# Six load buffers in place of three for the second MLP product, a last group of four pairs, and the output scale row made earlier

## The chip, the cores and the metric

The kernel runs on one core of a Trainium2 chip. The time is device microseconds of one execution. TensorE does the matrix products, VectorE and ScalarE the elementwise work, GpSimd issues accumulating DMAs, and SyncE issues the plain DMAs. [...]

## The reference, cut to what matters

One decoder layer for 512 tokens of width 1024, in float32. The change touches its last part, the MLP and its residual:

```python
h = rmsnorm(x, g_pre_ffn[l]) * (1.0 + sc2) + sh2
u = jax.nn.relu(h @ w_ff1[l])            # 512 x 4096
y = (u * u) @ w_ff2[l]                   # 512 x 1024
x = x + ga2 * rmsnorm(y, g_post_ffn[l])  # ga2: gate from w_ada and c
```

## The kernel before, in words

A product of two float32 matrices is made of three matmuls: each operand is split into a high part (float32r, copied by ScalarE) and a low part (the rest, subtracted by VectorE), and high x high, high x low and low x high are added in PSUM. `split` (line 112) is this pair of instructions.

The first product of the MLP, h @ w_ff1, takes 32 slabs of w_ff1 (tile `st`, 128x1024, a ring of three slots shared with all earlier loads), 24 matmuls each. Its squared results stay in SBUF as 16 blocks (`ub`). In the same loop, `ada_cols` computes the last eight columns of the gate; after the loop, `rows_of` (line 149) makes the row `ga2b` (gate times post-norm gain) out of them with eight transposes on TensorE into the two banks "tr", and VectorE copies the banks to SBUF.

The second product, (u*u) @ w_ff2, is the seven-product stage. It goes over 16 pairs of w_ff2 slabs. A pair is a 2 x 2 block matrix on both sides (two halves of the tokens, two slabs; two halves of the columns), and a scheme of seven products in place of eight is used, with sums of blocks as operands. It has two phases.

First phase: for each pair p, four products into the accumulators p1, p5, p6, p7 (two PSUM banks each; p1 has the banks "tr"), 24 matmuls. `first_ops(p)` makes the operands: the split of four token blocks (`ah`), the two column halves of slab 2p (`x`, loaded by `load(p)`), and a sum n. `w_right[p]` holds the right column halves of both slabs of the pair, and n is that plus x. For p = 0 to 2 (`BY_DVE`) the slab `w_right[p]` is loaded plainly and VectorE adds x to it (line 879); for p > 2 `column_sums(p)` (line 865) lets ScalarE copy x to a tile `wn` and GpSimd add `w_right[p]` to it with an accumulating DMA. `ah` has two tiles, one for even and one for odd pairs, and the weights `whi` and `wlo` four slots (`WBUF`), two for each pair. So the operands of pair p + 1 are made while TensorE multiplies pair p.

Second phase: three more products for each pair, 18 matmuls, onto the same accumulators. `fourth_sum(p)` (line 899) adds a half slab to a block with an accumulating DMA; `second_ops(p)` (line 902) splits the slab 2p + 1 (`w`), three token blocks (`a`) and that sum (`n`, a tile `wn`). The last `LAST` = 3 pairs are taken in another order: result tile by result tile (p7 for tokens 2 and 3, then p5 and p1 for tokens 0, then 1). As each of the six tiles is done, `piece` (line 996) takes it up on VectorE (L1001 adds, L1005 multiplies with `ga2b`) and ScalarE (square with a sum), and `end` (line 1012) applies the norm, adds the residual and stores.

Inside the stage the order on TensorE, VectorE, ScalarE and GpSimd is the order of the code (`manual_schedule`), and SyncE issues its loads in one queue, each waiting for its slot. An instruction that waits holds up all that is behind it on its engine. The program sets aside a part of SBUF for the descriptors of GpSimd's DMAs; before, its size is left at the default.

## Time and profile before

| | us |
|---|---|
| median of three runs | 801.88 (801.0 to 801.96) |
| profiled execution | 802.46 |
| its span, first to last instruction | 800.5 |
| TensorE busy | 767.6 (96%), 4014 matmuls |
| VectorE busy | 593.9 (74%) |
| ScalarE busy | 415.0 (52%) |
| mean granted clock | 0.993 |

A busy TensorE is one with matmuls in its pipe. The chain of work that ended last gives 71% of the span to TensorE, 17% to VectorE and 7% to DMA. Shares over the whole span hide that stages differ, so the rows below are read by stage. The w_ff1 product ends at about 631 us, the first phase of the seven-product stage goes from there to about 726 us, the second to the last matmul at 791.4 us.

### The profile page before, as it was taken

Reading aid. Unit: us, or ns where it says so; the run is one execution under the profiler, and the core shown is the slowest. Engines: PE = TensorE matmul, PEld = TensorE weight load, DVE = VectorE, ACT = ScalarE, POOL = GpSimd, SP = SyncE. Lnnn points to the kernel's source line nnn. Section 1 sums busy time; section 2 is a strip of 40 time slices with the busy share of each in tenths; the row PEclk is TensorE's granted clock in tenths of the full one; section 3 lists DMA queues with packets and bytes.
Section 4 is the critical chain, followed back from the end, with each engine's and each line's share of the span. In section 5 each row is a group of like instructions: output and inputs, shape, how many; then the busy total and the mean of one; then the engine's idle time right before and its main releaser. Section 6 shows DMA issues by size and latency. Waiting matters only on the chain.

```text
span 800.5 us, 10875 instructions
## 1 busy us (share of the span) xinstructions
PE 767.6 (96%) x4014; PEld 638.4 (80%) x4014; DVE 593.9 (74%) x1112; ACT 415.0 (52%) x752; POOL 28.3 (4%) x44
## 2 busy tenths in 40 slices
PE   5999999998899999998999999999999989999995
PEld 5889977667889887786788898888888858888884
DVE  6876799999957578678875964655544668887966
ACT  6555666554546668623245852232232258777852
POOL 0000000000000000000000000000000011142000
PEclk9999999999999999999999999999999999999998
DMA  9933201112122210377883234444332269899622
GB/s 352 386 121 106 79 27 54 54 63 95 55 82 77 80 54 27 102 247 247 271 298 123 79 130 133 141 150 137 128 103 71 74 150 211 204 195 268 198 77 105
DMA packets 32598, 111.18 MB, mean 139 GB/s; under 512 B 3873, under 2 KB 3873, under 8 KB 32545
## 3 DMA queue, kind: packets, MB, share of 16 engines
q1 hardware_dynamic: 28224, 99.44, 36.3%
q0 software_dynamic: 4176, 11.01, 8.2%
q8 instruction: 31, 0.51, 0.3%
q14 instruction: 23, 0.18, 0.1%
q10 hardware_dynamic: 144, 0.03, 0.0%
HBM read 108.38 MB, written 2.10 MB: 138 GB/s over the span
## 4 chain that ended last, share of the span: by engine, by line
PE 71%; DVE 17%; DMA 7%; issue 2%; ACT 2%; SPq 0%; DVEq 0%; ACTq 0%
PE mm L140 25%; PE s L140 19%; PE o L140 6%; PE s L858 6%; PE mm L858 5%; PE tr L858 4%; DMA st<-in_ada_dram 3%; DVE wlo L114 3%; DVE a L486 3%; DVE isc L412 2%; DVE sm L411 2%; DMA st<-in_w_gate_dram 2%; PE tr L430 2%; DVE be L488 1%; PE tr L140 1%
## 5 line engine op out<-in xcount | busy, mean ns | idle before, releaser
L113 ACT ACTIVATE whi<-st 128x1024 fp32r<-128x1024 f32 (+3 forms) x119 | 117.4, 989 | 170.8 <-DMA st<-in_w_up_dram 45.0
L114 DVE TENSOR_TENSOR wlo<-st,whi 128x1024 fp32r<-128x1024 f32 (+3 forms) x119 | 134.8, 1135 | 65.4 <-ACT whi L113 65.2
L140 PE MATMUL mm<-hTh,whi 128*128 128x512 f32 x192 | 78.2, 407 | 0.1
L140 PE MATMUL mm<-hTh,wlo 128*128 128x512 f32 x192 | 75.3, 392 | 0.0
L140 PE MATMUL mm<-hTl,whi 128*128 128x512 f32 x192 | 75.1, 391 | 0.0
L140 PE MATMUL mm<-whi,hTh 128*128 128x256 f32 (+2 forms) x208 | 62.6, 307 | 0.0
L213 DVE CUSTOM_DVE_ANT_0 st<-st,cb,vec 128x1024 f32<-128x1024 f32 x32 | 40.9, 1283 | 27.7 <-DMA st<-in_ada_dram 27.7
L140 PE MATMUL mm<-wlo,hTh 128*128 128x256 f32 (+2 forms) x208 | 60.5, 297 | 0.0
L140 PE MATMUL mm<-whi,hTl 128*128 128x256 f32 (+2 forms) x208 | 60.5, 297 | 0.0
L140 PE MATMUL s<-h2h,whi 128*128 128x512 f32 (+1 forms) x120 | 43.4, 361 | 0.0
L140 PE MATMUL s<-h2l,whi 128*128 128x512 f32 (+1 forms) x120 | 43.3, 361 | 0.0
L140 PE MATMUL s<-h2h,wlo 128*128 128x512 f32 (+1 forms) x120 | 43.3, 361 | 0.0
L140 PEld LDWEIGHTS mm<-hTh,wlo 128*128 128x128 f32 x192 | 36.0, 188 | 7.7
L140 PEld LDWEIGHTS mm<-hTh,whi 128*128 128x128 f32 x192 | 36.2, 189 | 6.6 <-DVE qT L524 0.3
L140 PEld LDWEIGHTS mm<-hTl,whi 128*128 128x128 f32 x192 | 36.2, 188 | 6.2
L140 PEld LDWEIGHTS mm<-wlo,hTh 128*128 128x128 f32 x208 | 40.0, 192 | 1.1
L140 PEld LDWEIGHTS mm<-whi,hTl 128*128 128x128 f32 x208 | 39.9, 192 | 0.6
L140 PEld LDWEIGHTS mm<-whi,hTh 128*128 128x128 f32 x208 | 39.5, 193 | 0.4
L858 PE MATMUL s<-whi,ah 128*128 128x512 f32 x100 | 36.3, 393 | 0.0
L114 DVE TENSOR_TENSOR ah<-ub,ah 128x1024 fp32r<-128x1024 f32 (+1 forms) x17 | 20.5, 1208 | 18.1 <-ACT ah L113 18.1
L140 PE MATMUL s<-kT,qT 128*128 128x256 f32 (+2 forms) x128 | 30.9, 346 | 2.1 <-ACT be L485 1.8
L868 POOL DMA_DIRECT2D wn<-in_w_right_dram x13 | 11.4, 876 | 594.3 <-ACT wn L867 551.2
(352 smaller groups left out, 1947.1 us busy)
## 6 DMA issues: line engine op xcount, KB each, us to landing
st<-in_w_ff_dram SPq DMA_DIRECT2D x64, 512.0 KB, 3.5
st<-in_ada_dram SPq DMA_DIRECT2D x32, 512.0 KB, 4.3
sa<-in_ada_dram SPq DMA_DIRECT2D x16, 512.0 KB, 8.2
st<-in_w_gate_dram SPq DMA_DIRECT2D x16, 512.0 KB, 3.3
wn<-in_w_right_dram POOLq DMA_DIRECT2D x13, 512.0 KB, 5.5
st<-in_w_first_dram SPq DMA_DIRECT2D x8, 512.0 KB, 8.7
st<-in_w_b_dram SPq DMA_DIRECT2D x8, 512.0 KB, 3.3
st<-in_w_a_dram SPq DMA_DIRECT2D x8, 512.0 KB, 3.2
```

What stands on the lines that cost most here:

```text
L113: nc.scalar.activation(dst_hi, src, AF.Copy)
L114: nc.vector.tensor_tensor(dst_lo, src, dst_hi.bitcast(F32), op=ALU.subtract)
L140: nc.tensor.matmul(o, lhsT, rhs, start=start, stop=stop)
L213: nc.vector.tensor_tensor_reduce(out=st, in0=st, in1=cb[0], scale=1.0, scalar=vec[:, j:j + 1], op0=ALU.mult, op1=ALU.add, accum_out=mod[:, ...
L411: nc.vector.max(out=m8, in_=cur)
L412: nc.vector.match_replace(out=cur, in_to_replace=m8, in_values=cur, imm_value=SENT)
L430: nc.tensor.transpose(tr[:, j * P:(j + 1) * P], ps[e][:, j * P:(j + 1) * P], ident)
L486: nc.vector.tensor_tensor_scan(a[:, n - 1::-1], a[:, n - 1::-1], zero.to_broadcast([P, n]), 1.0, op0=ALU.mult, op1=ALU.add)
L488: nc.vector.tensor_tensor(be[:, :n - 1], be[:, :n - 1], a[:, 1:n], op=ALU.mult)
L858: nc.tensor.matmul(acc[i], s[:, ts], m[:, cs], start=f, stop=l, skip_group_check=onto)
L868: nc.gpsimd.dma_start(nw[p], w_right[p], accum_op=ALU.add)
```

## The change

`w_right[0..2]` and the w_ff2 slabs now alternate between the old ring `st` (three slots) and a new ring `ld` (three slots) through `incoming`; loads are issued up to seven pairs ahead, column sums four pairs ahead in place of three, and the ring `wn` has four slots. Room for it comes from a descriptor space of 4 KB in place of the default, from `stat` living in the old gain tile `g1`, and from `jk` moving to another pool. The last group has four pairs. `second_ops` splits the token operands ahead of the slab, and in the loop p7 comes before p1 and p5. `rows_of(ga2b, ...)` is called inside the loop over w_ff1, as soon as the last gate column is there.

```diff
@@ constants
-LAST = 3
+LAST = 4
@@ loop over w_ff1
                     gated_gain(KT + i, 40 + i, 72 + i)
-        rows_of(ga2b, ga[:, KT:], evac)
+                    if i == KT - 1:
+                        rows_of(ga2b, ga[:, KT:], evac)
@@ seven-product stage
-            return f3p.tile([P, D], F32R, name=uid("wn"), tag="wn", bufs=3)
+            return f3p.tile([P, D], F32R, name=uid("wn"), tag="wn", bufs=4)
+        turns = [0]
+
+        def incoming(src):
+            turns[0] += 1
+            if turns[0] % 2:
+                return stage(src)
+            t = f2p.tile([P, D], F32, name=uid("ld"), tag="ld", bufs=3)
+            nc.sync.dma_start(t, src)
+            return t
+
         def load(j):
-            xw[j] = stage(w_ff2[2 * j]) if j < NP else stage(w_ff2[2 * (j - NP) + 1])
+            xw[j] = incoming(w_ff2[2 * j] if j < NP else w_ff2[2 * (j - NP) + 1])
@@ second_ops
-            split(w[0], w[1], y)
             split(ah, al, blk(p, 3, 3))
             split(n[:, H0], n[:, H1], t2)
+            split(w[0], w[1], y)
@@ first phase
-        for j in range(2):
+        for j in range(BY_DVE):
             load(j)
-            if j == 0:
-                nw[0] = stage(w_right[0])
+            nw[j] = incoming(w_right[j])
         first_ops(0)
-        nw[1] = stage(w_right[1])
-        load(2)
+        load(3)
+        load(4)
         for p in range(NP):
-            if p in (1, 2):
-                column_sums(p + 2)
             if p + 1 < NP:
                 first_ops(p + 1)
-            if p == 0:
-                nw[2] = stage(w_right[2])
-                load(3)
-            elif p == 1:
-                load(4)
-                load(5)
             if p == NP - 1:
                 second_ops(0)
-            if p > 1:
-                load(p + 4)
-                if p + 3 < NP:
-                    column_sums(p + 3)
+            if p < 2:
+                load(2 * p + 5)
+                load(2 * p + 6)
+            else:
+                load(p + 7)
+            if p == 0:
+                column_sums(3)
+            if p + 4 < NP:
+                column_sums(p + 4)
@@ second phase
-        jk = f3p.tile([P, 512], BF16, name="jk2")
-        stat = f3p.tile([P, LINE // 4], F32, name="stat")
+        jk = f2p.tile([P, 512], BF16, name="jk2")
+        stat = g1
-            if p + 4 < NP:
-                load(NP + p + 4)
-            for args in (on_p1, on_p5, on_p7):
+            if p + 7 < NP:
+                load(NP + p + 7)
+            for args in (on_p7, on_p1, on_p5) if p else (on_p1, on_p5, on_p7):
-        second_ops(NP - 1)
+        for p in range(NP - LAST + 2, NP):
+            second_ops(p)
@@ kernel
-    nc = bacc.Bacc("TRN2", target_bir_lowering=False, num_devices=1)
+    nc = bacc.Bacc("TRN2", target_bir_lowering=False, num_devices=1, dynamic_dma_scratch_size=4096)
```

SyncE before, from the last w_ff1 slab (st_5987) on: st_6049, st_6053, st_6073 and st_6093 are the slabs of pairs 0 to 3, with the three w_right slabs between them.

```order
L109 DMA st_5987<-in_w_ff_dram 128x1024
L109 DMA st_6049<-in_w_ff_dram 128x1024
L109 DMA st_6051<-in_w_right_dram 128x1024
L109 DMA st_6053<-in_w_ff_dram 128x1024
L109 DMA st_6071<-in_w_right_dram 128x1024
L109 DMA st_6073<-in_w_ff_dram 128x1024
L109 DMA st_6091<-in_w_right_dram 128x1024
L109 DMA st_6093<-in_w_ff_dram 128x1024
```

SyncE now, at the broadcast of c early in the w_ff1 loop:

```order
L109 DMA st_5131<-in_w_ff_dram 128x1024
L160 DMA cb_4781<-in_c_row_dram 128x1024
L870 DMA ld_6051<-in_w_right_dram 128x1024
L870 DMA ld_6055<-in_w_right_dram 128x1024
L870 DMA ld_6059<-in_w_right_dram 128x1024
L109 DMA st_5167<-in_w_ff_dram 128x1024
```

The three w_right slabs have moved past 32 loads of the w_ff1 loop, and from the last w_ff1 slab on the slabs of pairs 0 to 4 (st_6049 to ld_6079) follow one another:

```order
L109 DMA st_5999<-in_w_ff_dram 128x1024
L109 DMA st_6049<-in_w_ff_dram 128x1024
L109 DMA st_6053<-in_w_ff_dram 128x1024
L109 DMA st_6057<-in_w_ff_dram 128x1024
L109 DMA st_6077<-in_w_ff_dram 128x1024
L870 DMA ld_6079<-in_w_ff_dram 128x1024
L109 DMA st_6097<-in_w_ff_dram 128x1024
```

ScalarE before, from the last result of the w_ff1 product (L811) to the operands of pair 2 (ah_6122 on); wn_6119 is the column-sum copy of pair 3.

```order
L811 ACTIVATE ub_4776<-mm_5993 128x512
L113 ACTIVATE ah_6075<-ub_4762 128x1024
L113 ACTIVATE whi_6076<-ub_4762 128x512
L867 ACTIVATE wn_6119<-st_6093 128x1024
L113 ACTIVATE ah_6122<-ub_4763 128x1024
L113 ACTIVATE whi_6123<-st_6073 128x512
L113 ACTIVATE whi_6125<-st_6091 128x1024
L113 ACTIVATE whi_6123<-ub_4763 128x512
```

ScalarE now, at the same place; wn_6101 and wn_6104 are the column-sum copies of pairs 3 and 4.

```order
L811 ACTIVATE ub_4776<-mm_6005 128x512
L113 ACTIVATE ah_6081<-ub_4762 128x1024
L113 ACTIVATE whi_6082<-ub_4762 128x512
L878 ACTIVATE wn_6101<-st_6077 128x1024
L878 ACTIVATE wn_6104<-ld_6079 128x1024
L113 ACTIVATE ah_6131<-ub_4763 128x1024
L113 ACTIVATE whi_6132<-st_6057 128x512
L113 ACTIVATE whi_6134<-ld_6059 128x1024
L113 ACTIVATE whi_6132<-ub_4763 128x512
```

Two copies in place of one stand ahead of the operands of pair 2. TensorE before, at the end of the w_ff1 product (mm_5993 is its last result, tr_6041 the first result bank of pair 0):

```order
L140 MATMUL mm_5993<-h2l,whi_5989 128x512
L140 MATMUL mm_5993<-h2h,wlo_5990 128x512
L154 MATMUL tr_6023<-identr,ga 128x128 x4
L154 MATMUL tr_6029<-identr,ga 128x128 x4
L858 MATMUL tr_6041<-whi_6056,ah_6055 128x512
```

TensorE now, between the 26th and the 27th slab of w_ff1:

```order
L140 MATMUL mm_5783<-h2l,whi_5779 128x512
L140 MATMUL mm_5783<-h2h,wlo_5780 128x512
L154 MATMUL tr_5817<-identr,ga 128x128 x4
L154 MATMUL tr_5823<-identr,ga 128x128 x4
L140 MATMUL s_5834<-h2h,wx_5831 128x512
```

The eight transposes stand six slabs earlier, and pair 0 follows the last matmul of the w_ff1 product directly.

## Rows read from the trace of the kernel before

**Rows 1.** Stretches: length; busy PE, PEld, DVE, ACT, POOL; clock, DMA share, GB/s.
```profile
460.00:480.00 20.00, 20.00 (x161) 19.53 (x161) 13.71 (x26) 11.81 (x20) 0.00 (x0) 1.00 0.37 124
645.00:660.00 15.00, 12.61 (x45) 8.68 (x44) 11.17 (x15) 9.05 (x11) 1.73 (x2) 0.89 0.79 179
660.00:778.00 118.00, 118.00 (x522) 97.73 (x521) 98.27 (x125) 87.08 (x114) 22.71 (x26) 1.00 0.80 196
```

**Rows 2.** TensorE's timeline: start, duration, line, operands, count, [idle before, releaser].
```profile
630.48 1.03 PE L154 MATMUL tr<-identr,ga 128*128 128x128 f32 x8
...
631.95 0.47 PE L858 MATMUL tr<-whi,ah 128*128 128x512 f32 x1 [0.44 <-DVE ga2b L187]
...
644.72 0.50 PE L858 MATMUL tr<-whi,ah 128*128 128x512 f32 x1 [1.60 <-ACT whi L113]
...
646.06 0.79 PE L858 MATMUL tr<-wlo,ah 128*128 128x512 f32 x1 [0.84 <-DVE wlo L114]
...
655.18 0.50 PE L858 MATMUL tr<-wlo,ah 128*128 128x512 f32 x1 [0.84 <-DVE wlo L114]
...
660.90 0.39 PE L858 MATMUL tr<-whi,ah 128*128 128x512 f32 x1
```

**Rows 3.** The chain of waits: start, duration, what; one first-product tile.
```profile
625.20 5.44 PE mm L140 x24
```

**Rows 4.** TensorE's busy time and granted clock in two single microseconds.
```profile
646.00:647.00 1.00, 0.94 (x2) 0.50 0.85 152
656.00:657.00 1.00, 0.91 (x5) 1.00 1.00 201
```

**Rows 5.** SyncE's timeline, the third w_right load.
```profile
636.61 0.33 SPq L109 DMA_DIRECT2D st<-in_w_right_dram  x1
```

**Rows 6.** ScalarE's timeline ahead of product 2.
```profile
636.58 0.63 ACT L113 ACTIVATE whi<-ub 128x512 fp32r<-128x512 f32 x1 [3.59 <-DVE ub L883]
642.14 1.06 ACT L867 ACTIVATE wn<-st 128x1024 f32<-128x1024 f32 x1 [4.93 <-DMA st<-in_w_ff_dram]
```

**Rows 7.** DMA from 600 us: packets, MB, share; issues, KB, us to landing.
```profile
q0 software_dynamic: 4176, 11.01, 32.5%
...
wn<-in_w_right_dram POOLq DMA_DIRECT2D x13, 512.0 KB, 5.5
...
st<-in_w_right_dram SPq DMA_DIRECT2D x3, 512.0 KB, 3.4
```

**Rows 8.** VectorE's timeline at the start of the stage.
```profile
631.12 1.29 DVE L187 COPY ga2b<-tr 128x512 f32<-128x512 f32 x2 [2.62 <-PE tr L154]
...
648.26 1.23 DVE L114 TENSOR_TENSOR wlo<-st,whi 128x1024 fp32r<-128x1024 f32 x1 [0.40 <-ACT whi L113]
...
658.33 1.22 DVE L114 TENSOR_TENSOR ah<-ub,ah 128x1024 fp32r<-128x1024 f32 x1 [0.52 <-ACT ah L113]
...
663.35 1.23 DVE L114 TENSOR_TENSOR ah<-ub,ah 128x1024 fp32r<-128x1024 f32 x1 [0.53 <-ACT ah L113]
```

**Rows 9.** The timeline of the tail, TensorE and VectorE.
```profile
783.47 0.39 PE L858 MATMUL s<-whi,a 128*128 128x512 f32 x1
...
783.67 0.69 DVE L1001 TENSOR_TENSOR yg<-mm,u 128x512 f32<-128x512 f32 x1 [0.64 <-PE mm L858]
...
786.92 0.69 DVE L1001 TENSOR_TENSOR yg<-s,u 128x512 f32<-128x512 f32 x1
...
790.78 0.68 DVE L1001 TENSOR_TENSOR yg<-s,u 128x512 f32<-128x512 f32 x1
...
791.40 0.39 PE L858 MATMUL tr<-whi,a 128*128 128x512 f32 x1
...
794.02 0.68 DVE L1005 TENSOR_TENSOR yg<-tr,ga2b 128x512 f32<-128x512 f32 x1
```

**Rows 10.** The timeline, the first fourth sum and its first reader.
```profile
710.60 1.22 POOL L900 DMA_DIRECT2D ub<-in_w_ff_dram  x1
...
721.70 0.61 ACT L113 ACTIVATE wn<-ub 128x512 fp32r<-128x512 f32 x1
```

## The prediction

> **What bounds the kernel now.** I read the busy time by stretch first, then TensorE's timeline where that showed holes, then what filled the idle time of ScalarE, VectorE and SyncE at those holes, and last the tail. From 660 to 778 us TensorE is busy for all of 118.00 us, at the full granted clock [rows 1]: nothing outside TensorE can buy time there. Before it, from 645 to 660 us, it is busy for 12.61 of 15.00 us at a mean granted clock of 0.89 [rows 1]. The timeline shows the holes: 0.44 us before the first pair of the stage (VectorE's eviction of the scale row, ga2b), 1.60 and 0.84 us in pair 2, 0.84 us in pair 3 [rows 2]. Pair 4 begins at 660.90, and the first at 631.95 [rows 2]. A pair is 24 matmuls here, and 24 matmuls in a row take 5.44 us [rows 3], so four pairs want 21.76 us and got 28.95: 7.19 us are lost. [...]

> The large pauses come from SyncE. The load of the third w_right slab is issued only at 636.61 [rows 5], since it waits for one of the three slots of the ring "st", and the slab of pair 3 stands behind it. ScalarE stands still for 4.93 us until 642.14, since the copy for the column sum of pair 3 heads its queue [rows 6], and the operands of pair 2 are queued behind that copy.

> **The change part by part.**

> *Six buffers, and the order of the loads.* The three w_right slabs are now issued straight after the broadcast of c, near 466 us. There TensorE is busy 20.00 of 20.00 us and the DMA engines 0.37 [rows 1], so three more loads of 512 KB (3.4 us from issue to landing each [rows 7], one after another 10.2 us at the most) are hidden; were they not, one slab of w_ff1 would come later and find ScalarE's conversions far ahead. The slab of pair 3 no longer stands behind a w_right slab. It waits for slab 0's slot, which is free once the operands of pair 0 are made, before that pair's matmuls start. So the DMA wait of 4.93 us goes.

> What is late next? ScalarE and VectorE. The copies for the column sums of pairs 3 and 4 now both stand ahead of pair 2's operands on ScalarE; before, one did. In the trace the path from the start of that copy (642.14) to the end of the low half of pair 2's second weight operand on VectorE (648.26 plus 1.23) is 7.35 us [rows 6, 8], with no transfer in it; a second copy adds its 1.06 us, some of it overlapped, so I take 1.0. ScalarE is free for it when the last operand of pair 1 is split, 636.58 plus 0.63 = 637.2 [rows 6]. That start stays: the transposes delay the end of the w_ff1 product by 1.0 us, and VectorE is spared the eviction of 1.29 us [rows 8] in return. So the low half is ready at 637.2 + 7.35 + 1.0 = 645.55. TensorE asks for it with the eighth matmul of pair 2: at the stage's new start, 631.49 (below), plus two pairs (10.88) plus seven matmuls (1.59), 643.96. **A pause of 1.6 us stays** in pair 2. Its bounds: none, if the copies overlap better than I take it; 3.0 us, if both add in full and the operand chain slips as well. Pair 3 should find its operands: VectorE's low halves follow each other every 5.02 us (663.35 less 658.33, rows 8), so 650.57, and it asks at 651.0. From there 5.02 against 5.44 us gains a little with every pair.

> *The scale row inside the w_ff1 product.* The eight transposes (1.03 us, rows 2) move to behind the twenty-sixth w_ff1 slab; they take their TensorE time there all the same. The eviction moves too, and with it the 0.44 us. The stage begins at 630.48 + 1.01 = 631.49 in place of 631.95. Cost bounds of the new place: nothing, or up to VectorE's 1.3 us if the last gain came late; the program has no new wait at those transposes, so nothing.

> Start of the stage: pair 4 began at 660.90 and now begins at 631.49 + 21.76 + 1.6 = 654.85. **Gain 6.05 us.**

> *The last group of four pairs, and the order inside the pairs.* The matmuls are the same in number. What changes is the tail. Before, the last group gives 9 matmuls to each of six result tiles, 2.04 us each, and VectorE needs longer than that for each: it takes up the second tile at 783.67, the third at 786.92, the fifth at 790.78 and the sixth at 794.02 [rows 9]. The second tile was taken up 0.43 us after its last matmul (one matmul of 0.23 us before 783.47), the sixth's last matmul is at 791.40, so that tile was ready at 791.83 and waited 2.19 us. Now a tile is 12 matmuls, 2.72 us. Count from A, when the sixth is ready: the second is ready at A - 10.88, VectorE takes the third at A - 7.63 (3.25 later, as in the rows), is free for the fifth at A - 3.77 (3.86 later) and so waits for TensorE, which gives it at A - 2.72. From there to the sixth is 3.24 us in the rows: A + 0.52 in place of A + 2.19. **Gain 1.67 us**, between 0 (VectorE's work is set by something else) and 2.19 (no waiting at all). Four n buffers and four weight pairs are just held by the four pairs; the last weight split can start only when pair 11 is through, and 7.5 us of seven-product work stand between that and its first use.

> *The 4 KB scratch, the scale row's statistics in g1, jk moved.* No instruction changes; only space does. The trace shows no wait for descriptor space, so the cost has bounds: nothing, or the rival below. I take nothing.

> *The accumulating loads.* The sixteen fourth sums follow the last column sum on GpSimd, which now comes one pair (5.44 us) earlier against TensorE. The plain loads beside them run six deep in place of three, so they are wanted later; this only adds slack.

> Sum: 6.05 + 1.67 = 7.72 us. The profiled execution took 802.46 us around its span of 800.5; the median of the runs is 801.88. The same offset is in both kernels, so I take 801.88 - 7.7 = **794.2 us**.

> **The rivals.**

> *The clock falls again (797.2 us).* Pairs 2 and 3 took 16.18 us before; without 10.88 of work and the two pauses of 0.84 us inside them up to 3.6 remain, most of it from half clock. The pause of 1.6 us that stays could bring it down again; I price that at 3.0. For it: the fall came after pauses of 1.60 and 0.84 us with one matmul between [rows 2, 4]. Against: 0.84 us alone at 655.18 left the clock full at 656. [...]

> *The tail does not move (795.9 us).* If the chain of square, square root and reciprocal sets the tail, the 1.67 us are not gained. For it: VectorE follows on ScalarE there. Against: the six tiles come every 2.04 us and it takes 3.24 to 3.86.

> *No pause in pair 2 (792.6 us).* Then 1.6 us more are gained.

> *The burst lands late and pauses return (801.9 us, no change).* DMA share is 0.80 over 660 to 778 [rows 1]; if six-deep loads crowd the accumulating ones, half a microsecond per pair over fifteen pairs eats the gain. Against: the same bytes move, earlier.

> *The small scratch makes accumulating loads wait for one another (slower, 804 us).* Place: GpSimd's sixteen fourth sums. Before, they are issued from 710.60 [rows 10] on, many at once, and the first is read at 721.70 [rows 10]. In the changed kernel they start at 710.60 - 6.05 - 5.44 = 699.1 and the first is read near 715.6; each further one is wanted 4.08 us (18 matmuls) later, so the sixteen have 16.5 + 15 x 4.08 = 77.7 us, 4.86 each. If only one were in flight and took the 5.5 us of a 512 KB one [rows 7], the last would be 10.3 us late: 794.2 + 10.3. It decides from 4.86 us on. Against: no row of before shows GpSimd waiting for space, with 4176 packets in 29 transfers [rows 7], 144 each. I give it 0.06. [...]

> **How the numbers follow.** Forecast 0.55; clock 0.16; tail 0.08; no pause 0.11; no change 0.04; slower 0.06. The range takes in the forecast and the first three rivals, 791.8 to 797.4 (the low end adds the rest of the tail's 2.19 and 0.3 of the runs' spread, the high end 0.2 of that spread); outside stand the last two and a rest, some 0.15. A change under 0.2% (1.6 us) can't be told from none here. Faster by more: 0.55 + 0.16 + 0.08 + 0.11 = 0.90; same 0.04; slower 0.06.

> **What the profile after would show.** Right: SyncE's w_right loads near 466 us; no idle time of ScalarE put down to a DMA between 632 and 660; pair 4 (the 97th matmul of the stage) starting 23.4 us after the first; one pause of about 1.6 us before a matmul that reads a low half; in the tail VectorE waiting for TensorE before the fifth tile, and the last square root about 1.7 us nearer to the last matmul. Wrong: half clock after pair 2; a hole in TensorE after 660; GpSimd's instructions for the fourth sums longer or later than one pair (5.44 us) ahead; a tail as long as before.

## The result, and the profile after

The changed kernel takes **793.16 us** (median; 790.99 to 793.87), the kernel before 801.92 on the same chip: a ratio of 0.9888, 95% interval 0.9867 to 0.991. Forecast were 794.2 us, between 791.8 and 797.4.

Both profiled executions, cut at the same places of the program (starts on TensorE's timeline; us):

| segment | before | after | difference | forecast |
|---|---|---|---|---|
| start of the stage | 631.95 | 630.71 | -1.24 | -0.46 |
| pair 0 to pair 4 | 28.95 | 23.33 | -5.62 | -5.59 |
| pair 4 to the last matmul | 130.49 | 130.33 | -0.16 | 0 |
| last matmul to VectorE's last pair of operations | 3.41 | 2.00 | -1.41 | -1.67 |
| from there to the end of the span | 5.68 | 4.54 | -1.14 | 0 |
| span | 800.5 | 790.9 | -9.6 | -7.7 |

The two terms of the sum are there in nearly their forecast size. Two rows were not forecast: 0.8 us of the earlier start, and 1.14 us behind the last operation. The first is not shown to come from the change: in the changed kernel and its variants below that have the same program up to the stage, the stage began anywhere from 628.67 to 632.23. The second is the subject of the last two experiments.

The stretches after (columns as in [rows 1]):

```profile
460.00:480.00 20.00, 20.00 (x159) 19.41 (x158) 13.56 (x25) 11.81 (x20) 0.00 (x0) 1.00 0.60 205
645.00:660.00 15.00, 15.00 (x68) 12.42 (x67) 13.70 (x20) 11.92 (x16) 2.59 (x3) 1.00 1.03 258
660.00:770.00 110.00, 110.00 (x487) 91.09 (x486) 91.77 (x117) 80.97 (x107) 20.96 (x24) 1.00 0.72 177
```

From 645 to 660 us TensorE is now busy for all of 15.00 us at a granted clock of 1.00, the full one; [rows 1] had 12.61 at 0.89. Near 466 us the DMA share rose from 0.37 to 0.60 and TensorE lost nothing. TensorE's timeline after has only two pauses in the stage, both in pair 2; the last row is pair 4:

```profile
643.37 0.50 PE L859 MATMUL s<-whi,ah 128*128 128x512 f32 x1 [0.26 <-ACT whi L113]
644.63 0.50 PE L859 MATMUL s<-wlo,ah 128*128 128x512 f32 x1 [0.76 <-DVE wlo L114]
...
654.04 0.39 PE L859 MATMUL tr<-whi,ah 128*128 128x512 f32 x1
```

The two waits stand for the three of [rows 2]. ScalarE ahead of them:

```profile
635.75 0.63 ACT L113 ACTIVATE whi<-ub 128x512 fp32r<-128x512 f32 x1 [2.53 <-DVE ub L894]
636.29 1.04 ACT L878 ACTIVATE wn<-st 128x1024 f32<-128x1024 f32 x1
637.24 1.04 ACT L878 ACTIVATE wn<-ld 128x1024 f32<-128x1024 f32 x1
638.19 1.04 ACT L113 ACTIVATE ah<-ub 128x1024 fp32r<-128x1024 f32 x1
639.13 0.62 ACT L113 ACTIVATE whi<-st 128x512 fp32r<-128x512 f32 x1
642.26 1.06 ACT L113 ACTIVATE whi<-ld 128x1024 fp32r<-128x1024 f32 x1 [2.51 <-DVE ld L890]
```

The DMA wait of 4.93 us [rows 6] is gone, and the two copies stand ahead of pair 2's operands as forecast. A little ahead of the copies ScalarE is idle for 2.53 us: that gap is where the first experiment puts them. SyncE and GpSimd after:

```profile
465.19 1.37 SPq L870 DMA_DIRECT2D ld<-in_w_right_dram  x3
```
```profile
697.75 0.86 POOL L879 DMA_DIRECT2D wn<-in_w_right_dram  x1 [4.58 <-ACT wn L878]
698.29 8.46 POOL L911 DMA_DIRECT2D ub<-in_w_ff_dram  x9
```

The third w_right load, at 636.61 in [rows 5], is issued near 466 with the others. The fourth sums begin at 698.29 where [rows 10] had 710.60, and nine go out in one row, as before (8.44 us there). VectorE's last pair of operations before, which [rows 9] don't show:

```profile
794.81 1.42 DVE L1016 SCALAR_TENSOR_TENSOR x<-yg,sm,x 128x512 f32<-128x512 f32 x2
```

The tail after, TensorE's last matmul, ScalarE's last square and VectorE from the fifth tile on:

```profile
782.08 0.69 DVE L1009 TENSOR_TENSOR yg<-s,u 128x512 f32<-128x512 f32 x1 [0.97 <-PE s L859]
...
784.00 1.42 DVE L1024 SCALAR_TENSOR_TENSOR x<-yg,sm,x 128x512 f32<-128x512 f32 x2
...
784.37 0.39 PE L859 MATMUL tr<-whi,a 128*128 128x512 f32 x1
...
784.86 0.60 ACT L973 ACTIVATE jk<-tr 128x512 bf16<-128x512 f32 x1 [1.09 <-PE tr L859]
...
785.58 0.69 DVE L1013 TENSOR_TENSOR yg<-tr,ga2b 128x512 f32<-128x512 f32 x1 [0.16 <-ACT jk L973]
...
786.37 1.42 DVE L1024 SCALAR_TENSOR_TENSOR x<-yg,sm,x 128x512 f32<-128x512 f32 x2
```

In [rows 9] VectorE took the fifth tile at once and reached the sixth 2.62 us after the last matmul began (794.02 less 791.40). Now it waits 0.97 us for TensorE before the fifth, and reaches the sixth 1.21 us after the last matmul began.

### The profile page after: what moved, and what is told of

The parts are those of the page before. It is cut to its first block, busy times and chain, and to the rows that moved or that the text cites. A ratio compares the mean times of both kernels' runs of the same rounds, so it can differ in the third digit from the quotient of the medians.

```text
span 790.9 us, 10885 instructions
## 1 busy us (share of the span) xinstructions
PE 765.3 (97%) x4014; PEld 638.5 (81%) x4014; DVE 593.3 (75%) x1112; ACT 415.2 (53%) x752; POOL 28.2 (4%) x44
## 3 DMA queue, kind: packets, MB, share of 16 engines
q0 software_dynamic: 4176, 11.01, 8.1%
## 4 chain that ended last, share of the span: by engine, by line
PE 74%; DVE 15%; DMA 6%; ACT 2%; issue 2%; SPq 0%; DVEq 0%; ACTq 0%
PE mm L140 25%; PE s L140 19%; PE o L140 7%; PE s L859 6%; PE mm L859 5%; PE tr L859 5%; DMA st<-in_ada_dram 3%; DVE a L486 3%; DVE wlo L114 2%; DVE isc L412 2%; DVE sm L411 2%; DMA st<-in_w_up_dram 2%; PE tr L430 2%; DVE be L488 1%; PE tr L140 1%
## 5 line engine op out<-in xcount | busy, mean ns | idle before, releaser
L113 ACT ACTIVATE whi<-st 128x1024 fp32r<-128x1024 f32 (+3 forms) x102 | 102.2, 1005 | 161.2 <-DMA st<-in_w_up_dram 43.6
L114 DVE TENSOR_TENSOR wlo<-st,whi 128x1024 fp32r<-128x1024 f32 (+3 forms) x102 | 117.3, 1153 | 55.3 <-ACT whi L113 55.0
L812 DVE TENSOR_TENSOR ub<-ub 128x512 f32<-128x512 f32 (+1 forms) x36 | 22.4, 627 | 10.8 <-ACT ub L811 10.8
```

What stands on the lines that cost most here:

```text
L113: nc.scalar.activation(dst_hi, src, AF.Copy)
L114: nc.vector.tensor_tensor(dst_lo, src, dst_hi.bitcast(F32), op=ALU.subtract)
L812: nc.vector.tensor_tensor(u, u, u, op=ALU.mult)
```

## The experiments

A pause is idle time of TensorE in the profile. All distances from the last matmul are counted from its start. The expectations give the one to the second operation of VectorE's last pair, 0.67 us behind the row shown; 2.67 and 4.1 there are 2.00 and 3.41 here.

**1. The two copies in ScalarE's gap.**

```diff
+            if p == 1:
+                column_sums(3)
+                column_sums(4)
             split(h1[:, H1], l1[:, H1], t2)
...
-            if p == 0:
-                column_sums(3)
-            if p + 4 < NP:
+            if 0 < p and p + 4 < NP:
                 column_sums(p + 4)
```

> The changed kernel with the column sums of pairs 3 and 4 issued earlier, ahead of the last split of pair 1's operands, so that their two copies run in the 2.5 us in which ScalarE stands idle there (633.2 to 635.75 in the trace after). Theory (the pauses of 0.26 and 0.76 us in pair 2 come from the two copies ahead of pair 2's operands on ScalarE): both pauses go, pair 4 starts 21.8 to 22.0 us after pair 0 in place of 23.33, and the time falls by 1.4 us, to about 791.6 us. Rival (the operands of pair 2 are late because of VectorE's own work or of the tiles they are written to): pair 4 still starts 23.3 us after pair 0, time unchanged.

Measured: 791.29 us (789.52 to 792.39), ratio to before 0.9862 [0.9844, 0.988]. Pair 2 has no pause, so the two copies were its cause; but pair 4 starts 22.89 us after pair 0. That is a gain of 0.44 us; the time fell by more, which nothing in the trace ties to the edit. ScalarE's timeline shows what came next:

```profile
643.07 1.06 ACT L878 ACTIVATE wn<-st 128x1024 f32<-128x1024 f32 x1 [1.93 <-DMA st<-in_w_ff_dram]
644.03 1.04 ACT L113 ACTIVATE ah<-ub 128x1024 fp32r<-128x1024 f32 x1
```

The copy for pair 5's sum waits for its slab, ahead of pair 3's operands, and TensorE pauses in pair 3 (0.46 us before a low half at 646.99). This is a wait of the same kind as the one that the change removed, one pair later.

**2. In addition, later sums three pairs ahead.**

```diff
-            if 0 < p and p + 4 < NP:
-                column_sums(p + 4)
+            if 1 < p and p + 3 < NP:
+                column_sums(p + 3)
```

> The kernel of the experiment with the sums of pairs 3 and 4 in the gap, and in addition each later column sum is issued three pairs ahead, behind the operands of the next pair, in place of four pairs ahead. In that experiment the pauses left pair 2, and ScalarE then stood 1.93 us before the copy for the sum of pair 5, which waits for a slab, ahead of pair 3's operands. Theory: with the sum of pair 5 behind those operands no pause is left; pair 4 starts 21.8 us after pair 0 in place of 22.89 and 23.33, the time is 1.5 us below that of the changed kernel, 791.6 us or less. Rival (VectorE's 5 us a pair or the accumulated sum itself is late): pair 4 still starts 22.5 us or more after pair 0, or TensorE pauses at pair 5.

Measured: 791.13 us (790.53 to 792.08), ratio 0.9871 [0.9856, 0.9887]. Pair 4 starts 21.76 us after pair 0, which is four times 5.44, and the whole stage has no pause:

```profile
630.00:645.00 15.00, 15.00 (x68) 12.43 (x67) 11.41 (x16) 10.15 (x13) 1.88 (x2) 1.00 0.53 125
645.00:660.00 15.00, 15.00 (x67) 12.40 (x67) 13.08 (x18) 10.98 (x14) 2.59 (x3) 1.00 0.93 257
```

By its trace this version beats both kernels: 1.57 us less than the changed one in this segment, the others the same. The intervals of the ratios overlap (0.9867 to 0.991 against 0.9856 to 0.9887), so the times alone don't show it.

**3. The scale row at its old place.**

```diff
-                    if i == KT - 1:
-                        rows_of(ga2b, ga[:, KT:], evac)
+        rows_of(ga2b, ga[:, KT:], evac)
```

> The changed kernel with the scale row made after the loop over w_ff1 as before. Simple sum: the idle 0.46 us before the first pair comes back and the time rises by 0.46 us, to 793.6 us. Second theory (ScalarE and VectorE make pair 2's operands at a time set by themselves, so a later stage only shortens the pauses in pair 2): pair 4 starts 22.9 us after pair 0 in place of 23.33, and the time is the same within 0.1 us.

Measured: 792.91 us (792.21 to 794.98), ratio 0.9888 [0.9871, 0.9906], the same as with the row moved. Pair 4 starts 22.93 us after pair 0, as the second theory had it. In this kernel the moved row buys 0.46 us at the start of the stage, and pair 2 gives 0.40 of it back (23.33 less 22.93), because its operands are made at a time that ScalarE and VectorE set.

**4. Three load buffers and the old order of loads and column sums.** Cut to its first parts:

```diff
         def incoming(src):
-            turns[0] += 1
-            if turns[0] % 2:
-                return stage(src)
-            t = f2p.tile([P, D], F32, name=uid("ld"), tag="ld", bufs=3)
-            nc.sync.dma_start(t, src)
-            return t
+            return stage(src)
...
+            if p in (1, 2):
+                column_sums(p + 2)
             if p + 1 < NP:
                 first_ops(p + 1)
+            if p == 0:
+                nw[2] = stage(w_right[2])
+                load(3)
```

> The changed kernel with the old ring of three load buffers and the old order of loads and column sums; the small descriptor space, the last group of four, the early scale row and the new order within the pairs stay. Theory (the gain of the stage's start comes from the loads): the 4.9 us wait of ScalarE for a transfer comes back, the clock falls to half in pair 2, pair 4 starts 28.9 us after pair 0 in place of 23.33, time up by 5.6 us to about 798.7 us. Rival (a good part of the gain came from the early scale row or from the start of the stage): less than 4 us.

Measured: 799.76 us (796.64 to 801.93), ratio 0.9965 [0.9952, 0.9978]; 6.6 us above the changed kernel. Pair 4 starts 30.50 us after pair 0: the loads carry the gain of the start, and more than I expected. What the buffers and what the order of the loads give by itself is not tried apart. ScalarE, then the stretch behind it:

```profile
642.83 1.06 ACT L873 ACTIVATE wn<-st 128x1024 f32<-128x1024 f32 x1 [6.09 <-DMA st<-in_w_ff_dram]
```
```profile
645.00:660.00 15.00, 13.59 (x42) 9.94 (x43) 11.21 (x14) 9.00 (x12) 1.95 (x3) 0.69 0.74 175
```

The wait is 6.09 us where [rows 6] had 4.93, 1.16 us longer: the slab of pair 3 landed 6.3 us after its issue, against 5.1 before. With the start of the stage 0.46 us earlier (experiment 3) that makes 1.62, about the 1.55 us by which 30.50 exceeds the 28.95 of the kernel before. Why the slab landed later stays open.

**5. and 6. A last group of three pairs, and of two.**

```diff
-LAST = 4
+LAST = 3
```

> The changed kernel with a last group of three pairs in place of four. Theory (VectorE takes longer for a result tile than TensorE for 9 matmuls, 2.04 us, but not much longer than for 12, 2.72 us): the last operation of VectorE starts 4.1 us after the last matmul in place of 2.67, the time rises by 1.4 us to about 794.6 us. Rival (the chain of square, square root and reciprocal after the last matmul sets the tail): 2.67 us and the time stay.

> The changed kernel with a last group of two pairs, 6 matmuls or 1.36 us to a tile. Theory (VectorE's 3.2 to 3.9 us a tile bound the tail): the queue of tiles grows by about 2.7 us more than with three pairs, the last operation of VectorE starts 6.8 us after the last matmul, the time rises by 4.1 us to about 797.3 us. Rival (tail set by the chain after the last matmul): as with four pairs, no change.

Measured: 794.4 us (792.42 to 796.63), ratio 0.9903 [0.9887, 0.992], with three; 797.32 us (794.82 to 797.77), ratio 0.9937 [0.9922, 0.9952], with two. VectorE's last operation started 4.08 and 6.79 us after the last matmul. Both are as the theory had them. VectorE's last rows with two pairs:

```profile
783.84 0.68 DVE L1013 TENSOR_TENSOR yg<-tr,ga2b 128x512 f32<-128x512 f32 x1
784.44 0.68 DVE L1009 TENSOR_TENSOR yg<-s,u 128x512 f32<-128x512 f32 x1
785.16 0.69 DVE L1013 TENSOR_TENSOR yg<-yg,ga2b 128x512 f32<-128x512 f32 x1
785.98 0.15 DVE L171 TENSOR_SCALAR sm<-sm 128x1 f32<-128x1 f32 x1
786.16 0.16 DVE L177 RECIPROCAL sm<-sm 128x1 f32<-128x1 f32 x1
786.36 1.41 DVE L1024 SCALAR_TENSOR_TENSOR x<-yg,sm,x 128x512 f32<-128x512 f32 x2
787.69 0.68 DVE L1013 TENSOR_TENSOR yg<-tr,ga2b 128x512 f32<-128x512 f32 x1
```

Not one of them shows a wait: the last matmul began at 782.36, and VectorE has yet to take the fourth tile then.

**7. The old order inside the pairs of the second phase.**

```diff
+            split(w[0], w[1], y)
             split(ah, al, blk(p, 3, 3))
             split(n[:, H0], n[:, H1], t2)
-            split(w[0], w[1], y)
...
-            for args in (on_p7, on_p1, on_p5) if p else (on_p1, on_p5, on_p7):
+            for args in (on_p1, on_p5, on_p7):
```

> The changed kernel with the slab split first in the second phase and the products in the old order p1, p5, p7. Theory (the last group of four needs the operands in the new order): a pause of TensorE of 1 to 1.5 us before the last group's fourth pair, time up by that. Rival (there is slack of several microseconds): no pause, same time.

Measured: 792.75 us (792.37 to 794.76), ratio 0.9885 [0.9868, 0.9902]. TensorE pauses once, 0.25 us before the sum's matmuls of the last group's fourth pair at 772.49, and from pair 4 to the last matmul 0.55 us more pass. That lies between the two expectations; the time doesn't show it. The 0.16 us of the table's third row have the same place: in the kernel before, the weight load of such a sum waits 0.28 us for VectorE at 780.83.

**8. to 10. The descriptor space:** 512 and 1024 bytes in the changed kernel, and 4 KB alone in the kernel before.

```diff
-dynamic_dma_scratch_size=4096
+dynamic_dma_scratch_size=512
```

> The changed kernel with a descriptor space of 512 bytes in place of 4 KB. [...] Rival (space does not bind): same issue times as with 4 KB. Second rival (only one in flight): the fourth sums come late, pauses of TensorE in the second phase, 10 us slower.

> The changed kernel with a descriptor space of 1024 bytes. With 512 bytes each accumulating load was issued only after the one before had landed, 7.5 us apart in the first phase and 4.1 us in the second. Theory (the space holds loads in proportion to its size): with 1024 bytes two are under way, they follow each other in 4 us or less, TensorE does not wait for them, the time is that of the changed kernel within 1 us. Rival (still one at a time): 834 us again.

> The kernel before with a descriptor space of 4 KB and nothing else changed. Theory (the space costs nothing): same as before, 801.9 us, GpSimd's fourth sums issued from 710.6 us on in one go as before. Rival (a small space makes accumulating loads wait for one another): slower by 2 us or more, fourth sums issued further apart.

Measured: with 512 bytes 834.15 us (832.35 to 836.16), ratio 1.0397 [1.0375, 1.0418]; with 1024 bytes 791.78 us (791.3 to 792.34), ratio 0.9879 [0.9864, 0.9893]; the kernel before with 4 KB 802.52 us (801.21 to 805.98), ratio 1.0007 [0.9994, 1.002]. GpSimd's timeline with 512 bytes:

```profile
645.25 0.89 POOL L879 DMA_DIRECT2D wn<-in_w_right_dram  x1 [7.18 <-ACT ah L113]
652.73 0.88 POOL L879 DMA_DIRECT2D wn<-in_w_right_dram  x1 [6.58 <-issue]
...
746.37 0.87 POOL L911 DMA_DIRECT2D ub<-in_w_ff_dram  x1 [3.14 <-issue]
750.42 0.87 POOL L911 DMA_DIRECT2D ub<-in_w_ff_dram  x1 [3.18 <-issue]
```

In these rows, but for the first, each load waits 6.6 or 3.2 us for nothing that the profile shows, and is issued 7.5 or 4.0 us after the one before it. One needs 7.2 or 3.8 us (medians) to land, so one is under way at a time. The second rival named the mechanism and priced it too low, since it had only the fourth sums: the column sums are paced too, at 7.5 us for a pair of 5.44. From pair 4 to pair 16 the program takes 90.74 us in place of 65.28, and 80.31 in place of 65.05 from there to the last matmul. With 1024 bytes, GpSimd's timeline from the last column sum on, then the time from issue to landing of that sum and of the first fourth sum:

```profile
697.03 0.87 POOL L879 DMA_DIRECT2D wn<-in_w_right_dram  x1 [4.56 <-ACT wn L878]
697.57 2.12 POOL L911 DMA_DIRECT2D ub<-in_w_ff_dram  x2
702.74 0.87 POOL L911 DMA_DIRECT2D ub<-in_w_ff_dram  x1 [3.05 <-issue]
706.27 0.86 POOL L911 DMA_DIRECT2D ub<-in_w_ff_dram  x1 [2.66 <-issue]
```
```profile
wn<-in_w_right_dram POOLq DMA_DIRECT2D x1, 512.0 KB, 5.4
ub<-in_w_ff_dram POOLq DMA_DIRECT2D x1, 256.0 KB, 8.4
```

The column sum and two fourth sums go out at once, three loads. The next goes out at 702.74, behind the landing of the first of them (697.03 + 5.4), and the one after at 706.27, behind that of the second (697.57 + 8.4). So three are under way at a time, not the two of the expectation. The last is issued at 733.17 (718.70 with 4 KB), TensorE waits for none, and from pair 4 on the segments are those of the changed kernel. With 4 KB and with the default, eight are under way before GpSimd waits, and that wait names a releaser, a landing. In the changed kernel the first of the nine landed 7.3 us after its issue, at 705.6, before the ninth went out at 705.89, and the wait is:

```profile
708.43 0.86 POOL L911 DMA_DIRECT2D ub<-in_w_ff_dram  x1 [1.68 <-DMA ub<-in_w_ff_dram]
```

**11. and 12. The end of the span.** In the kernel before, the last store's stretch, queues and the store's landing (median us), then the same of the changed kernel:

```profile
q14 instruction: 1, 0.01, 0.5%
issues: line engine op xcount, KB each, median us to landing
out_dram<-x SPq DMA_DIRECT2D x1, 256.0 KB, 3.2
```
```profile
q1 hardware_dynamic: 288, 0.52, 42.5%
issues: line engine op xcount, KB each, median us to landing
out_dram<-x SPq DMA_DIRECT2D x1, 256.0 KB, 2.0
```

Beside the last store of the kernel before stands one transfer of instructions (8 KB), and the store lands 3.2 us after its issue, not 2.0. Two kernels move that fetch without touching the end. The first cuts SyncE's first load into eight pieces:

```diff
-        nc.sync.dma_start(vec, vecs)
+        for i in range(8):
+            nc.sync.dma_start(vec[:, 11 * i:11 * i + 11], vecs[:, 11 * i:11 * i + 11])
```

> The kernel before with the first load of the program, of the vectors, cut into eight pieces: SyncE has seven more instructions at the start, nothing else changes. In the two traces with that program an instruction fetch of 8 KB starts 2.4 us before the end of the span, while the last store is under way, and the last landing comes 1.16 us after the others; in the eight traces of the changed program the fetch is 4.4 us or more ahead of the end and no landing is late. Theory (the fetch belongs to SyncE and delays a part of the last store): the fetch moves by several instructions, and VectorE's last operation is followed by 3.1 us in place of 4.27. Rival (the fetch belongs to another engine, or does not cause the delay): 4.27 us as before.

Measured: 804.24 us (803.33 to 806.86), ratio 1.0049 [1.0029, 1.0069]. The fetch still starts 2.5 us before the end, and 4.24 us follow VectorE's last operation, as the rival had it. So seven more instructions in SyncE's program don't move it. The kernel became 0.5% slower; its stage began at 633.18, and why is not shown.

```diff
+        idle = per.tile([P, 32], F32, name="idle")
+        for i in range(16):
+            nc.scalar.activation(idle[:, i:i + 1], eps, AF.Copy)
+            nc.vector.tensor_copy(idle[:, 16 + i:17 + i], eps)
```

> The kernel before with sixteen more one-column copies on ScalarE and sixteen on VectorE at the very start, where both engines wait for the first load; their results are not used. Cutting SyncE's first load left the instruction fetch 2.5 us before the end of the span and the last landing 1.04 us late. Theory (the fetch belongs to ScalarE's or VectorE's program, and its place in time sets whether the last store is late): the fetch moves to 4 us or more before the end, no landing is late, and VectorE's last operation is followed by 3.1 us in place of 4.27; nothing else changes but a few tenths of a microsecond at the start. Rival (the fetch sits at the end of the program whatever stands ahead of it): 4.2 us as before.

Measured: 803.98 us (802.41 to 805.5), ratio 1.0017 [1.0001, 1.0033]. The fetch starts 6.89 us before the end, and 3.17 us follow VectorE's last operation, as the theory had it. The last store's stretch has no instruction transfer:

```profile
q1 hardware_dynamic: 288, 0.52, 44.2%
issues: line engine op xcount, KB each, median us to landing
out_dram<-x SPq DMA_DIRECT2D x1, 256.0 KB, 2.1
```

The time did not fall by it: the stage began later (634.73), and from 733 us on its matmuls stood 0.232 us apart in place of 0.227, at a granted clock of 1.00, which cost 1.5 us in that profile and which I can't explain. So what is shown is the 1.1 us of the segment, not a faster kernel.

## Why the prediction was right

- *Six buffers.* This term was right in mechanism and size. Pair 4 came 23.33 us after pair 0 (forecast 23.36), without the wait for a transfer. The pause of 1.6 us that was to stay came as two, 0.26 and 0.76 us; a pause counts only the time after a matmul has left the pipe, and from start to start pair 2 took 7.01 us in place of 5.44. Experiment 1 shows that the two copies are its cause, experiment 4 that the loads carry the gain. Experiment 2 shows what the pause was worth, 1.57 us.
- *The scale row.* The forecast added the terms up to the start of pair 4, with the time fixed at which pair 2's operands are ready, and experiment 3 confirms that: of the 0.46 us at the start, 0.06 are left behind pair 2.
- *The last group.* VectorE took the third tile at 777.18 and the fifth at 782.08, forecast (with A = 784.80) 777.17 and 782.08. The sixth came at A + 0.78, not A + 0.52: the step "From there to the sixth is 3.24 us in the rows" was mis-sized, for VectorE waited 0.16 us for ScalarE's square of the same bank, and ScalarE had waited for TensorE. The gain was 1.41 us, not 1.67. Experiments 5 and 6 bear the tail out at three sizes.
- *One sign was named wrongly.* The last square root was to come 1.7 us nearer to the last matmul; it came 0.46 nearer (793.07 less 791.40, now 785.58 less 784.37). Before, ScalarE did not wait for VectorE there; the reciprocal behind it on VectorE came 1.40 us nearer (3.22 to 1.82).
- *The clock stayed full* in the changed kernel, so the first rival fell: its window had 1.00. At the start of the stage half clock followed pauses of 1.60 and 0.84 us before [rows 2, 4], 1.69 and 0.84 in the kernel before with 4 KB, 3.31 and 0.54 in experiment 4: the mean from 645 to 660 us was 0.89, 0.77 and 0.69. It did not follow 0.26 and 0.76 in the changed kernel, nor a single 0.74 in experiment 3, and not 1.47 and 0.85 in experiment 11 or 1.79 and 0.84 in experiment 12: there the mean was 1.00. So it was not certain for the long pauses either.
- *The scratch* cost nothing (the kernel before with 4 KB: 1.0007). But the rival was better founded than its 0.06 shows: the mechanism exists, and at 512 bytes costs 41 us. Its sum looked at the wrong loads. One at a time, sixteen fourth sums were issued 4.46 us apart on average, less than the 4.86 from which on they were to be late, but the first went out at 736.52 in place of 698.29, behind late column sums. The runs had one load under way in 512 bytes, three in 1024 and never more than eight in 4 KB; how many 4 KB would hold, none of them shows.
- *What was not forecast:* 1.14 us at the end, by where the program's instruction fetch fell, and 0.8 us ahead of the stage, within the spread of its start. Without them the profiled gain is 7.7 us, the forecast 7.72. That they agree so well is in part luck: the tail gave 0.26 us too little, and the order inside the pairs gave 0.16 that were put at nothing.

*What the half clock cost was read wrongly.* The prediction puts most of the 3.6 us that pairs 2 and 3 lost beside their two pauses of 0.84 us down to half clock, and prices its first rival by that at 3.0. In experiments 11 and 12, which run the stage of the kernel before, the clock stayed full, and the loss was the same. TensorE in pair 2 of experiment 12, and the stretch:

```profile
647.69 0.50 PE L862 MATMUL tr<-whi,ah 128*128 128x512 f32 x1 [1.79 <-ACT whi L117]
649.03 0.50 PE L862 MATMUL tr<-wlo,ah 128*128 128x512 f32 x1 [0.84 <-DVE wlo L118]
```
```profile
645.00:660.00 15.00, 9.88 (x36) 6.19 (x36) 9.65 (x12) 8.95 (x11) 1.88 (x2) 1.00 0.62 135
```

The granted clock from 645 to 660 us was 0.89 in the kernel before, 0.77 in it with 4 KB, 0.69 in experiment 4, and 1.00 in experiments 11 and 12; pairs 2 and 3 took 16.19, 16.23, 16.15, 16.13 and 16.08 us. They wait for their operands at either clock. The sum does not use this reading.

## What to carry to other kernels

Price a stall that goes by what is next in the same queue: here the two copies behind it kept 1.6 of the 7.2 us, and moving them into an idle gap of the same engine brought the rest only once the wait behind them was moved as well. In a tail where one engine takes the results of another in turn, write down when each piece is ready and when it is taken; forecast so, two of three times came out within 0.01 us. When a size has a cliff, run the sizes below the one you use: a quarter of the descriptor space cost nothing here and an eighth 41 us, and nothing in the profile of either kernel tells it. And before you put a loss down to a slower clock, look for a run in which the same stretch had the full clock.

## What the runs showed of the hardware

Half clock cost nothing that shows in pairs 2 and 3, where TensorE waits for operands anyway: the two took 16.08 to 16.23 us at a mean granted clock of 0.69 to 1.00. Much the same two pauses (1.60 and 0.84 us, 1.79 and 0.84) were followed by half clock in one execution (0.50 at 646 us) and not in another (1.00 from 645 to 660 us).

Where an instruction fetch of 8 KB fell beside the last store, the store landed 1.1 to 1.2 us later: so in the three traces with the fetch 2.4 to 2.5 us before the end (4.24 to 4.28 us from VectorE's last operation to the end), and in none of the eleven with it 4.3 us or more ahead of the end (3.12 to 3.17). In the three, a last packet of the store starts only when the 0.31 us of the fetch are over; that is less than the delay, and the rest is not explained.
